# First MLP of a two-layer trunk: 22 of 32 up units by seven block products, h kept in DRAM, conditioning in wide pieces beside down

## The chip, the core and the metric

The kernel runs on one core of one Trainium2 chip. The metric is the device time of one execution in microseconds (us). The kernel before took 2450.26 us, the median of three runs (2447.16 to 2452.15). Below, PE is the matrix engine, DVE the vector engine, ACT the scalar engine, POOL the GpSimd engine and SP the engine that issues the transfers.

## What is computed

One inference step of a trunk of two layers on 1056 tokens (1024 of a prompt, 32 of a sample) with a model width of 1024. Layer 0 is an mLSTM mixer, layer 1 an attention over a band of keys that are computed once; each is followed by a squared-ReLU MLP of 4096 hidden units. Shift, scale and gate of every part come from a conditioning vector `c`, one for the prompt and one for the sample. Cut to what matters here:

```
def trunk(x, c, ...):
    for l in range(DEPTH):
        sh1, sc1, g1, sh2, sc2, g2 = jnp.split(ada_mod(c, p['w_ada'][l], p['b_ada'][l])[:, None, :], 6, axis=-1)
        u = x * (1 + sc1) + sh1
...
            kv_shift, kv_scale = jnp.split(ada_mod(c, p['w_ada_kv'], p['b_ada_kv'])[:, None, :], 2, axis=-1)
            kv = (x * (1 + kv_scale) + kv_shift) @ p['w_kv']
            q = (u @ p['w_q_b'][lb]).reshape(Bsz, S, NH_B, HD_B)
...
        x = layer_norm(ALPHA * x + (1 + g1) * y, p['ln_g'][l, 0], p['ln_b'][l, 0])
        u = x * (1 + sc2) + sh2
        f = jnp.square(jax.nn.relu(u @ p['w_up'][l])) @ p['w_down'][l]
        x = layer_norm(ALPHA * x + (1 + g2) * f, p['ln_g'][l, 1], p['ln_b'][l, 1])
```

So the queries and keys of layer 1 need the norm behind the first MLP, and that norm's output is modulated by the conditioning of layer 1 (`w_ada[1]`, 48 columns of 128) and of the keys and values (`w_ada_kv`, 16 columns).

## The kernel before

All data lie with the 1024 features on 128 partitions by 8 (`KC`), tokens along the free axis. Tokens are cut into three blocks of 384, 384 and 288 (`TBS`), or into four quarters of 264 (`QN`). A product in fp32 is made of three matmuls on numbers split into a high and a low part: high times high, high times low, low times high (`proj`, L118 to L120). ACT writes the high part of a weight block and DVE the low part (`split`, L89 and L90); the split weights lie in a ring of six slots ("wc"), the raw ones in a ring of three ("raw"). `U` holds the split, modulated input of the current stage.

**The first MLP** is `mlp` in `make_layer`. The 4096 hidden units are taken in 8 groups of 512. Up of group g+1 is interleaved with down of group g. An up tile is 24 matmuls into a PSUM bank; ACT and DVE take relu, square and split it (L1025 to L1028), and h stays in SBUF. A down tile is 12 matmuls; DVE adds it with the gate to the residual `acc`, which lies in one tile for each block of tokens (`add_gated_at`, L986). In the last group the block of 384 tokens comes first, then three up tiles that were kept back, then the other two blocks; when a block is complete, its norm starts (`norm`, L864 to L896), whose last step writes the block's part of `U` (L331) for the q projection.

**The conditioning** of layer 1 is `ada_cols`: 32 steps of two columns. A step loads two pieces of 512 KB, multiplies and adds them on DVE in rows of 256 (L238 and L241, 14 and 2 of them), transposes (L245) and sums (L246) on DVE; every fourth step PE sums across the partitions (L252). A `Flow` hands out these steps beside the matmuls: every tile "ticks" it by a share of its width, and `finish` runs what is left at once. The conditioning begins with the third block's first up tile and is finished ahead of the first block's norm.

**The second MLP** is already `mlp7`: of its 32 units of 256 hidden units by 528 tokens, 22 are computed by seven products of half blocks in place of eight (`Seven`, L1300, 12 matmuls each of 264 columns), ten plainly (four tiles of 24 matmuls); the sums and differences that this needs are made by DVE and ACT (`forms`, L1303 to L1310), and h goes through DRAM (`hd`). Its down is also made of such products (L1409).

The order of the instructions on each engine is fixed when the program is built; an engine runs its own in that order.

## Time and profile before

| what | value |
|---|---|
| median of three runs | 2450.26 us |
| the profiled execution's own time | 2451.64 us |
| its span in the trace | 2449.7 us |
| granted TensorE clock, mean | 0.993 |
| PE busy | 2386.9 us |
| DVE busy | 1919.8 us |
| ACT busy | 1090.7 us |
| moved by DMA | 335.15 MB |
| first MLP, from its first up matmul to the first q matmul | 518.4 to 1266.9 us |
| first up matmul of the second MLP | 1730.8 us |

Rows of the trace read so: a group has the line, the engine, the operation, the tile written and the tiles read with their shapes, and how often; then its busy time and the mean of one in ns; then how long the engine stood idle ahead of it and what ended that. A window's row has the window, its length and, for each engine, the busy time with the number of instructions; then the mean granted clock, the busy share of the DMA engines and GB/s.

### The profile page before, as it was taken

What the parts mean: (1) busy time and instruction counts of PE and PEld (TensorE: products, weight loads), DVE (VectorE), ACT (ScalarE), POOL (GpSimd) and SP (SyncE); (2) the same over time, 40 slices, a digit from 0 to 9 for tenths busy, and PEclk for the clock granted to TensorE, in tenths of its full rate; (3) what the DMA queues carried; (4) which work ended last, traced back from release to release, by engine and by line L of the source; (5) the groups of instructions that cost most, each with busy time, mean ns of one, the idle gap of its engine ahead of it and who ended that gap; (6) DMA issues with size and microseconds to landing.
All of it is one profiled execution on the core that took longest, in us unless ns stands there. A gap on an engine that the chain in (4) does not pass through costs nothing.

```text
span 2449.7 us, 42910 instructions
## 1 busy us (share of the span) xinstructions
PE 2386.9 (97%) x16580; PEld 2294.7 (94%) x16580; DVE 1919.8 (78%) x4340; ACT 1090.7 (45%) x2264; POOL 167.3 (7%) x315
## 2 busy tenths in 40 slices
PE   7999999999999999999999999999999999899997
PEld 4999999999999999999999977789999999899997
DVE  4899998788678678687488666755998888887878
ACT  4554456283212212212157466763776777222212
POOL 0211100000000000000000224420000000000003
PEclk9999999999999999999999999999999999999999
DMA  7432223412233233233223230041486779966642
GB/s 287 137 102 88 89 80 109 157 35 87 89 101 121 87 104 113 82 116 107 89 77 101 64 73 2 10 117 42 159 275 233 255 256 335 376 234 230 228 156 72
DMA packets 251503, 335.15 MB, mean 137 GB/s; under 512 B 12824, under 2 KB 201644, under 8 KB 250276
## 3 DMA queue, kind: packets, MB, share of 16 engines
q1 hardware_dynamic: 251300, 332.42, 41.4%
q8 instruction: 130, 2.13, 0.4%
q14 instruction: 73, 0.60, 0.1%
HBM read 255.50 MB, written 79.24 MB: 137 GB/s over the span
## 4 chain that ended last, share of the span: by engine, by line
PE 76%; DVE 12%; DMA 4%; ACT 3%; issue 2%; POOL 0%; SPq 0%; ACTq 0%; DVEq 0%; POOLq 0%
PE dn L1409 11%; PE up L1300 6%; PE up L118 6%; PE up L120 6%; PE up L119 6%; PE dn L119 5%; PE dn L118 5%; PE dn L120 5%; PE pv L1749 3%; PE s L1692 2%; PE pt L1727 2%; PE o L118 1%; PE o L119 1%; PE o L120 1%; DMA hd<-HL 1%
## 5 line engine op out<-in xcount | busy, mean ns | idle before, releaser
L1409 PE MATMUL dn<-fx,wf_d 128*128 128x264 f32 x2016 | 254.2, 285 | 6.9 <-DVE ACX L986 3.3
L1409 PEld LDWEIGHTS dn<-fx,wf_d 128*128 128x128 f32 x2016 | 248.7, 188 | 9.3 <-issue 2.9
L119 PE MATMUL dn<-h,w_dn 128*128 128x384 f32 (+1 forms) x768 | 249.5, 325 | 0.0
L118 PE MATMUL up<-U,w_up 128*128 128x384 f32 (+1 forms) x768 | 249.2, 324 | 0.0
L119 PE MATMUL up<-U,w_up 128*128 128x384 f32 (+1 forms) x768 | 247.9, 323 | 0.0
L118 PE MATMUL dn<-h,w_dn 128*128 128x384 f32 (+1 forms) x768 | 247.8, 323 | 0.0
L120 PE MATMUL up<-U,w_up 128*128 128x384 f32 (+1 forms) x768 | 247.6, 322 | 0.0
L120 PE MATMUL dn<-h,w_dn 128*128 128x384 f32 (+1 forms) x768 | 247.3, 322 | 0.0
L986 DVE SCALAR_TENSOR_TENSOR ACX<-dn,ada,ACX 128x264 f32<-128x264 f32 (+5 forms) x400 | 160.1, 426 | 52.6 <-PE dn L1409 39.6
L238 DVE SCALAR_TENSOR_TENSOR aacc<-rada,cs,aacc 128x256 f32<-128x256 f32 x448 | 190.1, 476 | 0.0
L986 DVE SCALAR_TENSOR_TENSOR acc<-dn,ada,acc 128x384 f32<-128x384 f32 (+2 forms) x256 | 119.2, 485 | 47.0 <-PE dn L120 45.6
L1025 ACT ACTIVATE r<-up 128x384 f32<-128x384 f32 (+1 forms) x96 | 44.3, 463 | 243.3 <-PE up L120 236.9
L119 PEld LDWEIGHTS dn<-h,w_dn 128*128 128x128 f32 x768 | 144.5, 188 | 0.2 <-DVE h L1028 0.2
L120 PEld LDWEIGHTS dn<-h,w_dn 128*128 128x128 f32 x768 | 144.5, 188 | 0.0
L120 PEld LDWEIGHTS up<-U,w_up 128*128 128x128 f32 x768 | 144.3, 188 | 0.0
L118 PEld LDWEIGHTS up<-U,w_up 128*128 128x128 f32 x768 | 144.2, 188 | 0.1
L119 PEld LDWEIGHTS up<-U,w_up 128*128 128x128 f32 x768 | 144.2, 188 | 0.0
L118 PEld LDWEIGHTS dn<-h,w_dn 128*128 128x128 f32 x768 | 143.9, 187 | 0.2
L1300 PE MATMUL up<-u,wf_u 128*128 128x264 f32 x1056 | 139.6, 284 | 1.3 <-ACT wf_u L89 0.6
L1300 PEld LDWEIGHTS up<-u,wf_u 128*128 128x128 f32 x1056 | 132.6, 188 | 1.9 <-ACT wf_u L89 0.8
L1027 DVE TENSOR_TENSOR r<-r 128x384 f32<-128x384 f32 (+1 forms) x96 | 49.9, 522 | 103.3 <-ACT h L1026 102.9
L89 ACT CAST w_up<-raw_up 128x1024 fp32r<-128x1024 f32 x52 | 54.3, 1046 | 136.4 <-DMA raw_up<-in_w_up_dram 102.5
(386 smaller groups left out, 6575.0 us busy)
## 6 DMA issues: line engine op xcount, KB each, us to landing
rada<-in_w_ada_dram SPq DMA_DIRECT2D x64, 512.0 KB
hd<-HL SPq DMA_DIRECT2D x28, 1056.0 KB
raw_up<-in_w_up_dram SPq DMA_DIRECT2D x52, 512.0 KB
fx<-hd SPq DMA_DIRECT2D x50, 528.0 KB
hd<-HM SPq DMA_DIRECT2D x28, 792.0 KB
raw_dn<-in_w_down_dram SPq DMA_DIRECT2D x36, 512.0 KB
ada_room<-in_w_ada_dram SPq DMA_DIRECT2D x32, 512.0 KB
rdn_u<-in_w_up_dram SPq DMA_DIRECT2D x32, 512.0 KB
```

The source lines that it names most:

```text
L89: nc.scalar.copy(dst_h, src)
L118: nc.tensor.matmul(ps, wh, mov(0, k), start=(k == 0), stop=False)
L119: nc.tensor.matmul(ps, wh, mov(1, k), start=False, stop=False)
L120: nc.tensor.matmul(ps, wl, mov(0, k), start=False, stop=(k == nk - 1))
L238: nc.vector.scalar_tensor_tensor(acc[:, cnd], raw[:, k], sc, acc[:, cnd], op0=ALU.mult, op1=ALU.add)
L986: nc.vector.scalar_tensor_tensor(xs, ps[:, off + o:off + o + mm_], gate[:, fc, cnd:cnd + 1], xs, op0=ALU.mult, op1=ALU.add)
L1027: nc.vector.tensor_mul(r, r, r)
L1300: nc.tensor.matmul(p, self.ws[w][:, wl, k], moving(f, tp, xl, k), start=first and k + n_ == 0, stop=k == 3 and n_ == 2, skip_group_check=n ...
L1409: nc.tensor.matmul(p, ws[w][:, wl, k], t[:, s0, xl], start=first and k + n_ == 0, stop=k == kg - 1 and n_ == 2, skip_group_check=not first)
L1692: nc.tensor.matmul(s[:, b, :w], qst, kk[i][:, g, k0 + j0:k0 + j0 + w], start=(i == 0), stop=(i == 1))
L1727: nc.tensor.transpose(pt[:kp, j - j0, pr * P:(pr + 1) * P], ps_[pr][:, j * P:j * P + kp], ident)
L1749: nc.tensor.matmul(pv[64 * e:64 * e + 64, :nq], V[:kp, vt0 + j, g * 64:(g + 1) * 64], pts[e][:kp, j, :nq], start=(j == 0), stop=(j == nt - 1))
```

## The change

- `mlp` is gone. The first MLP runs by `mlp7(L0)` with `nw = 0`. All of up comes first: ten units plainly (the hidden blocks 6 to 15 on the first 528 tokens, 40 tiles of 24 matmuls of 264 columns), 22 units by seven products of 12 matmuls.
- Every h is written to DRAM (`hpl0`) and read again: for five of the eight groups of down into strips of `U`, for the other three (1, 4, 7) into tiles of a pool of their own (`hs`).
- Down is plain, eight groups (the hidden blocks in the order 0, 3, 1, 4, 2, 5, 7, 6): five of them in quarters of 264 tokens, three in the blocks of 384, 384 and 288. In the last group the loop runs over the blocks outside, and each block's norm follows its last tile. No up tile is left by then.
- The residual is two tiles of four feature rows over all tokens (`Halves`). It goes to DRAM (`xsp[3]`) after the norm ahead of the MLP and is loaded again (`reload`, tiles `ACX`), because scratch of the seven products lies in its place.
- Conditioning: eight columns of `w_ada_kv` stay narrow and run beside the seven products (`ada_some`). The 48 columns of `w_ada[1]` and the other eight of `w_ada_kv` run beside down in `ada_wide`: 14 steps of four columns, rows of 512, two pieces of 1 MB a step, which take slots of the "wc" ring. `finish` stands ahead of the first block's norm again.

```diff
+    def ada_wide(src, c0, base, nch, mk, tmp_f, raw_f, step):
+        for j in range(0, nch, 4):
+            acc = [tmp_f([P, 512], f"aw_{base}_{j}_{cnd}") for cnd in range(2)]
+            for half in range(2):
+                raw = raw_f([P, 4, 512], f"radw_{base}_{j}_{half}")
...
+                yield step[0]
+                for k in range(4):
+                    for cnd in range(2):
+                        sc = cs[:, 4 * half + k, cnd:cnd + 1]
+                        if half or k:
+                            nc.vector.scalar_tensor_tensor(acc[cnd], raw[:, k], sc, acc[cnd], op0=ALU.mult, op1=ALU.add)
+                        else:
+                            nc.vector.tensor_scalar(acc[cnd], raw[:, k], sc, None, op0=ALU.mult)
...
+        if not NW:
+            L.reload(3)
+            L.down()
+            for c in range(4):
+                h_load(1, c)
+            for g in range(8):
+                if g < 7:
+                    for pr in range(4):
+                        w_plain(g, pr)
+                        if g < 6 and pr:
+                            for c in ((0, 1), (2,), (3,))[pr - 1]:
+                                h_load(g + 2, c)
+                        for fc in (2 * pr, 2 * pr + 1):
+                            for t0, n in TBS if g % 3 == 1 else blocks_p:
+                                dn_plain(g, fc, t0, n)
+                else:
+                    for pr in range(4):
+                        w_plain(g, pr)
+                    for t0, n in L.blocks:
+                        for fc in range(KC):
+                            dn_plain(g, fc, t0, n)
+                        L.after((t0, n))
...
+    def ada_some():
+        yield from ada_cols(a["w_ada_kv"], 0, 96, 8, mm, tmp_t, ADA_B)
     def ada_rest():
-        yield from ada_cols(a["w_ada"][1], 0, 48, 48, mm, tmp_t, ADA_B)
-        yield from ada_cols(a["w_ada_kv"], 0, 96, 16, mm, tmp_t, ADA_B)
+        yield from ada_wide(a["w_ada"][1], 0, 48, 48, mm, tmp_t, wc_tile, ADA_W)
+        yield from ada_wide(a["w_ada_kv"], D, 104, 8, mm, tmp_t, wc_tile, ADA_W)
...
-    mlp(hp, 0, ada_part(0, 5), fwd, before0, end0, TBS)
...
+        def after(blk):
+            t0, n = blk
+            ti = TBS.index(blk)
+            flow.finish(norms["ada"])
+            norms[ti] = flow.add(norm(ti, 1, f"n01_{ti}", W01, False, lambda ti: acc_dma(
+                xsp[1][:, :, t0:t0 + n], acc[ti], True)), now=NOW)
+    mlp7(L0)
```

**First place: DVE at the end of the first MLP.** Before, the last rows of the conditioning (`aacc_96_14` is the last step's sum) stand beside the down tiles of group 6 (`dn_0_6_…`, group, feature row, first token):

```order
L986 SCALAR_TENSOR_TENSOR acc0_2_5244<-dn_0_6_1_768_12063,ada_87,acc0_2_5244 128x32
L238 SCALAR_TENSOR_TENSOR aacc_96_14_12028<-rada_96_14_1_12101,cs_86,aacc_96_14_12028 128x256 x4
L986 SCALAR_TENSOR_TENSOR acc0_0_5252<-dn_0_6_2_0_12083,ada_87,acc0_0_5252 128x384
L245 STREAM_TRANSPOSE aat_96_14_12168<-aacc_96_14_12028 128x512
L90 TENSOR_TENSOR w_dn0_6_2_12211<-raw_dn0_6_2_12209,w_dn0_6_2_12211 128x1024
L986 SCALAR_TENSOR_TENSOR acc0_1_5248<-dn_0_6_2_384_12103,ada_87,acc0_1_5248 128x384
L246 TENSOR_REDUCE cx_117<-aat_96_14_12168 128x16
```

Also before, a group later on DVE, the first block's norm (`s_n01_0` is its first sum) stands among and right behind that block's last adds, and relu and split of an up tile follow (`r`, `h`):

```order
L867 TENSOR_TENSOR s_n01_0_12724<-acc0_0_5252 128x768
L986 SCALAR_TENSOR_TENSOR acc0_0_5252<-dn_0_7_4_0_12663,ada_87,acc0_0_5252 128x384
L986 SCALAR_TENSOR_TENSOR acc0_0_5252<-dn_0_7_5_0_12677,ada_87,acc0_0_5252 128x384
L869 TENSOR_TENSOR s_n01_0_12724<-s_n01_0_12724,acc0_0_5252 128x768
L986 SCALAR_TENSOR_TENSOR acc0_0_5252<-dn_0_7_6_0_12696,ada_87,acc0_0_5252 128x384
L986 SCALAR_TENSOR_TENSOR acc0_0_5252<-dn_0_7_7_0_12710,ada_87,acc0_0_5252 128x384
L869 TENSOR_TENSOR s_n01_0_12724<-s_n01_0_12724,acc0_0_5252 128x768
L870 TENSOR_TENSOR s_n01_0_12724<-s_n01_0_12724 128x384
L90 TENSOR_TENSOR sr_n01_0_12729<-s_n01_0_12724,sr_n01_0_12729 128x384
L1027 TENSOR_TENSOR r_0_7_3_384_12757<-r_0_7_3_384_12757 128x384
L1028 TENSOR_TENSOR h_0_7_3_12556<-r_0_7_3_384_12757,h_0_7_3_12556 128x384
```

Now, on DVE, the two last conditioning steps (`aw_104_0` and `aw_104_4`, of `w_ada_kv`) begin behind an add of the last group's third block (tokens from 768):

```order
L1034 SCALAR_TENSOR_TENSOR ACX0_0_9705<-dn0_7_3_768_14367,ada_88,ACX0_0_9705 128x256
L1034 SCALAR_TENSOR_TENSOR ACX0_0_9705<-dn0_7_3_768_14367,ada_88,ACX0_0_9705 128x32
L267 TENSOR_SCALAR aw_104_0_0_13995<-radw_104_0_0_13997,cs_87 128x512
L267 TENSOR_SCALAR aw_104_0_1_13996<-radw_104_0_0_13997,cs_87 128x512
L265 SCALAR_TENSOR_TENSOR aw_104_0_0_13995<-radw_104_0_0_13997,cs_87,aw_104_0_0_13995 128x512
L265 SCALAR_TENSOR_TENSOR aw_104_0_1_13996<-radw_104_0_0_13997,cs_87,aw_104_0_1_13996 128x512
```

and only when both are through does the first block's norm begin:

```order
L272 STREAM_TRANSPOSE awt_104_4_0_14115<-aw_104_4_0_14093 128x512
L272 STREAM_TRANSPOSE awt_104_4_1_14118<-aw_104_4_1_14094 128x512
L274 TENSOR_REDUCE cx_118<-awt_104_4_0_14115 128x2x8
L274 TENSOR_REDUCE cx_118<-awt_104_4_1_14118 128x2x8
L915 TENSOR_TENSOR s_n01_0_14152<-ACX0_0_9705 128x768
L288 TENSOR_TENSOR ada_88<-adas_104_6_14121,pt2_86 128x16
L917 TENSOR_TENSOR s_n01_0_14152<-s_n01_0_14152,ACX0_1_10391 128x768
L299 TENSOR_SCALAR ada_88<-ada_88 128x16
L1034 SCALAR_TENSOR_TENSOR ACX0_1_10391<-dn0_7_5_768_14428,ada_88,ACX0_1_10391 128x256
```

Between the first of these rows and the norm's first stand 40 rows of the two steps: 28 of L265, four of L267, four transposes, four sums. So the end of the conditioning moved from a group ahead of the norm to directly ahead of it, behind nearly all the adds of all three blocks.

**Second place: PE at the same point.** Before, the first mean of the norm stands between up tiles that were kept back:

```order
L119 MATMUL up_0_7_2_768_12762<-U_133,w_up0_7_1_1_12498 128x288
L120 MATMUL up_0_7_2_768_12762<-U_133,w_up0_7_1_1_12498 128x288
L864 MATMUL mean_n01_0_12792<-sr_n01_0_12729,ones_d_73 128x384 x2
L118 MATMUL up_0_7_3_768_12814<-U_133,w_up0_7_1_0_12493 128x288
L119 MATMUL up_0_7_3_768_12814<-U_133,w_up0_7_1_0_12493 128x288
```

Now, on PE, the conditioning's sums over partitions (`adas_104_6`) and the mean stand behind the tile `dn0_7_6_768`:

```order
L119 MATMUL dn0_7_6_768_14452<-hs_0_7_3_13263,w_dn0_7_3_13934 128x288
L120 MATMUL dn0_7_6_768_14452<-hs_0_7_3_13263,w_dn0_7_3_13934 128x288
L285 MATMUL adas_104_6_14121<-cx_118,sel_69 32x16 x4
L912 MATMUL mean_n01_0_14202<-sr_n01_0_14157,ones_d_73 128x384
L118 MATMUL dn0_7_6_384_14266<-hs_0_7_0_13001,w_dn0_7_3_13934 128x384
L912 MATMUL mean_n01_0_14202<-sr_n01_0_14157,ones_d_73 128x384
```

Behind `adas_104_6` the matmuls left of the first MLP are those of three tiles, `dn0_7_6_384`, `dn0_7_4_768` and `dn0_7_7_768`, 36 in all; between the add's tile `dn0_7_3_768` and `adas_104_6` there are two tiles, `dn0_7_5_768` and `dn0_7_6_768`, 24 matmuls.

**Third place: DVE at the start of down.** The low half of the weights of feature rows 4 and 5 of group 0 (`w_dn0_0_2`) now stands behind all adds of row 3, and PE's next tile reads it:

```order
L1034 SCALAR_TENSOR_TENSOR ACX0_0_9705<-dn0_0_3_264_10618,ada_88,ACX0_0_9705 128x264
L1034 SCALAR_TENSOR_TENSOR ACX0_0_9705<-dn0_0_3_528_10636,ada_88,ACX0_0_9705 128x264
L1034 SCALAR_TENSOR_TENSOR ACX0_0_9705<-dn0_0_3_792_10650,ada_88,ACX0_0_9705 128x232
L1034 SCALAR_TENSOR_TENSOR ACX0_0_9705<-dn0_0_3_792_10650,ada_88,ACX0_0_9705 128x32
L90 TENSOR_TENSOR w_dn0_0_2_10667<-raw_dn0_0_2_10665,w_dn0_0_2_10667 128x1024
L1034 SCALAR_TENSOR_TENSOR ACX0_1_10391<-dn0_0_4_0_10672,ada_88,ACX0_1_10391 128x264
```

There is no such place in before, whose first down tiles have up tiles between them; the same order holds once more for `w_dn0_0_3` behind the adds of row 5. In the groups from 2 on, the weights stand two to ten tiles ahead.

313 lines of the change are left out of this document (161 added, 152 removed).

## The prediction

> **What bounds the kernel now.** I read the page's busy times and the chain of work that ended last first:
>
> ```profile
> span 2449.7 us, 42910 instructions
> PE 2386.9 (97%) x16580; PEld 2294.7 (94%) x16580; DVE 1919.8 (78%) x4340; ACT 1090.7 (45%) x2264; POOL 167.3 (7%) x315
> PE 76%; DVE 12%; DMA 4%; ACT 3%; issue 2%; POOL 0%; SPq 0%; ACTq 0%; DVEq 0%; POOLq 0%
> ```
>
> PE is the bound over the whole, but a share of 97% says nothing of one stage. So next come the windows of the first MLP, and the rows of its matmuls and of the first q matmuls behind it:
>
> ```profile
> 518.30:1266.80 748.50, 748.46 (x4683) 746.09 (x4683) 555.64 (x1194) 203.93 (x354) 0.00 (x0) 1.00 0.30 93
> L118 PE MATMUL up<-U,w_up x768: 288/336/443, 518.4 to 1236.0; 128*128 128x384 f32 x128, 128*128 128x288 f32 x64
> L118 PE MATMUL dn<-h,w_dn x768: 292/334/443, 577.0 to 1266.5; 128*128 128x384 f32 x128, 128*128 128x288 f32 x64
> L118 PE MATMUL q<-U,w_q x192: 288/336/447, 1266.9 to 1362.3; 128*128 128x384 f32 x128, 128*128 128x288 f32 x64
> ```
>
> In this stage PE is busy for 748.46 of 748.50 us, at full clock, with DVE at 555.64 (74%). Nothing waits: the stage costs exactly its matmuls, and the first q matmul starts 0.4 us after the last down matmul. What the change can gain here is matmul columns only, and every wait that it makes is new. With three lines each of 768 matmuls, up has 2304 and down 2304, of 352 columns on average, in all 1,622,000 columns in 748.5 us: **0.4615 ns a column**, so 121.8 ns for one of 264.
>
> The end of the stage matters as much. The waits of PE from 1200 to 1420 us (microseconds in all, times, longest), then three rows of DVE's timeline (start, duration) of the first block's norm:
>
> ```profile
> PE kv L1644 <- DVE uk L90: 3.0, 3, 1.9
> PE q L118 <- DVE QO L1573: 0.5, 1, 0.5
> PE q L118 <- ACT U L326: 0.2, 1, 0.2
> ```
>
> ```profile
> 1226.30 0.96 DVE L869 TENSOR_TENSOR s_n<-s_n,acc 128x768 f32<-128x768 f32 x1
> ...
> 1253.52 0.56 DVE L331 TENSOR_TENSOR U<-ut_n,U 128x384 fp32r<-128x384 f32 x1
> ...
> 1267.72 0.55 DVE L331 TENSOR_TENSOR U<-ut_n,U 128x384 fp32r<-128x384 f32 x1
> ```
>
> From the block's last sum to the first row of `U` pass 27.2 us, to the last 41.4 us, and PE hardly waits (0.7 us ahead of q), since it has three up tiles and two blocks of group 7 to do meanwhile. That cover is what I look for in the changed order.
>
> **Up, by columns.** Ten plain units have 10 × 4 tiles × 24 = 960 matmuls, 22 units of seven products have 22 × 7 × 12 = 1848, that is 84 a unit in place of 96. In all 2808 of 264 columns: 2808 × 0.1218 = 342.0 us, against 2304 × 352 × 0.4615 ns = 374.3 before: **−32.3**. Down keeps its columns, 374.3 us.
>
> **Up, by waits.** The second MLP has exactly this stage already:
>
> ```profile
> 1725.00:1854.00 129.00, 122.00 (x973) 120.86 (x973) 125.46 (x169) 94.26 (x150) 0.00 (x0) 0.99 0.67 226
> 1854.00:2083.50 229.50, 227.92 (x1863) 226.87 (x1862) 201.55 (x347) 165.80 (x290) 0.00 (x0) 1.00 0.79 272
> ```
>
> It takes 358.5 us, 16.5 over its columns, 7.0 of them idle PE in the first window, where DVE is busy for 125 of 129 us. Here DVE has less to do beside the products: h is only split, with no differences of h to form, and the conditioning beside them is four narrow steps. I take +5, between 0 and that stage's 16.5, nearer to the low end as the first window's idle comes of a full DVE. That h goes through DRAM I cost at nothing: the second window moves 272 GB/s at a share of 0.79 with PE idle for 1.6 us of 229.5.
>
> **Down, by waits.** DVE now carries twelve of the fourteen wide steps here. The rows for their prices:
>
> ```profile
> L238 DVE SCALAR_TENSOR_TENSOR aacc<-rada,cs,aacc 128x256 f32<-128x256 f32 x448 | 190.1, 476 | 0.0
> L241 DVE TENSOR_SCALAR aacc<-rada,cs 128x256 f32<-128x256 f32 x64 | 19.9, 342 | 0.0
> L245 DVE STREAM_TRANSPOSE aat<-aacc 128x512 f32<-128x512 f32 x32 | 22.6, 705 | 0.3
> L246 DVE TENSOR_REDUCE cx<-aat 128x16 f32<-128x512 f32 x32 | 21.7, 678 | 0.2
> L986 DVE SCALAR_TENSOR_TENSOR acc<-dn,ada,acc 128x384 f32<-128x384 f32 x128 | 78.3, 612 | 35.1 <-PE dn L120 34.1
> L986 DVE SCALAR_TENSOR_TENSOR ACX<-dn,ada,ACX 128x264 f32<-128x264 f32 x200 | 96.7, 488 | 31.0 <-PE dn L1409 28.2
> L90 DVE TENSOR_TENSOR w_dn<-raw_dn,w_dn 128x1024 fp32r<-128x1024 f32 x36 | 43.6, 1213 | 15.4 <-ACT w_dn L89 15.4
> ```
>
> No row has 512 columns with a scalar from `cs`. From 264 to 384 columns the same operation gains 124 ns, 1.03 ns a column, so 512 take 744 ns alone; in a run, 448 rows of 476 ns took 190.1 us, 424 each, so 52 ns of each hide under its neighbour: 692 ns. A wide step is 14 × 0.692 + 2 × 0.45 (L241's price, with another 256 columns) + 2 × 0.705 + 2 × 0.68 = 13.4 us, two steps 26.7; without overlap 28.4. In 6.3 groups of down (295 us of PE) DVE's order has twelve steps (160 us), 29 weight splits (35) and some 240 adds (92 with the same overlap), 287 us: **97% full**, where this stage had 74%. In such a stretch the second MLP's first window lost 7 us of 129. Most of DVE's work here is not urgent, though, so I take +4, from 0 to 15. At the start of down two weight splits stand behind adds of the tile just ahead of their first use: one split of ACT and DVE, some 2 us of PE each, **+4** (0 to 6).
>
> **The tail.** This is the term that decides. In DVE's order the two last conditioning steps stand behind the add of `dn0_7_3_768`, and the norm's first row behind them. What PE still has in that time is two tiles, 24 matmuls of 288 columns, 3.2 us. Then it stands at `adas_104_6`, which needs the second step's sums. Add 0.6 us, two steps 26.7 to 28.4 us, less 3.2: **24.4 us** of idle PE (24 to 26). In before these rows cost nothing, since a whole group of matmuls covered them.
>
> Then the norm of the first block starts, 45 DVE rows up to the first `U`. Its wide rows:
>
> ```profile
> L877 DVE TENSOR_TENSOR acc<-acc,mean_n 128x768 f32<-128x768 f32 x16 | 14.5, 947 | 2.4 <-PE mean_n L864 2.4
> L881 DVE TENSOR_TENSOR q_n<-q_n,q_n 128x768 f32<-128x768 f32 x18 | 17.1, 952 | 0.2
> L896 DVE TENSOR_TENSOR acc<-acc,w_n 128x768 f32<-128x768 f32 x16 | 14.9, 950 | 0.0
> ```
>
> There are 19 such rows (0.95 us each, 18.1), since the second block's sums and centring stand between; five weight splits for q at 1.21 (6.1); and small rows and adds, some 9 at the prices above. With the overlap of some 50 ns a row that is 30 us, and some 2 for the ways from DVE to ACT and PE and back. It agrees with the 27.2 us of before's timeline. PE's cover is 36 matmuls (12 × 177 + 24 × 133 ns = 5.3 us) and the norm's own, 1: **+26** (22 to 30). The rest of `U` comes over another 11 us, in which PE can take only the rows that are there, and the second block's over 21 more, which five or six q tiles of 4.2 us cover: **+4** (2 to 8).
>
> And PE that waited comes back slow:
>
> ```profile
> PE var_n L864 <- ACT qr_n L89: 4.1, 1, 4.1
> 1700.00:1750.00 50.00, 45.91 (x299) 45.45 (x298) 46.70 (x89) 35.90 (x70) 0.00 (x0) 0.97 0.28 87
> ```
>
> After the one wait of 4.1 us the window's granted clock is 0.97, 1.5 us of 50. The tail ends with waits at least that long: +1.5. [...]
>
> Tail: 24.4 + 26 + 4 + 1.5 = **56** (50 to 62).
>
> **Sum.** −32.3 + 5 + 4 + 4 + 56 = +36.7 on the profiled execution's 2451.64: **2488 us**. The median shown is 1.4 lower, which is within the runs' own spread.
>
> **Rivals.**
>
> *The tail is covered (faster).* If PE had matmuls for the tail as in before, with 4 us of waits between 1200 and 1420, the sum would be −32.3 + 13 + 4 = −15, 2436 us. The point from which it decides: the tail's idle under 19 us, the gain less the other waits. For it speaks that before hid the same 27 us of norm nearly whole. Against it: the orders are fixed, and with 60 matmuls behind that add the two steps alone pass 19 us. Chance 0.04.
>
> *Only the conditioning is paid.* If the norm's chain runs shorter and the three tiles left cover more of it (a tail of 30 in place of 56), the sum is +11, 2462. Against it stands that the norm's rows have prices seen twice, in groups and timeline. Chance 0.08.
>
> *DVE becomes the bound of down.* At 97% in a fixed order each late row delays the next add, PSUM banks stay taken and PE stops: +15 in place of 4, and up at the second MLP's 16.5: 2488 + 11.5 + 11 = 2511; with the one alone 2499. For it: the window with DVE at 125 of 129. Chance 0.15.
>
> *The products don't save what they should.* If forms and splits come too late all through, up loses 32 in place of 5 and is no faster than before: 2515. Against it, the second MLP's later window is 99% busy. Chance 0.05.
>
> The forecast itself: 0.68.
>
> **How the numbers follow.** The lowest bounds of all terms give 2451.64 − 32.3 + 50 = 2469, the highest 2451.64 − 32.3 + 16.5 + 15 + 6 + 62 = 2519; that all are at their highest is unlikely, and with one of the waits of up and down at its middle it is 2512. I give 2468 to 2512, which leaves out the covered tail, the conditioning alone and half of the fourth rival, some 0.15, and a little of the third. About 0.2% (5 us) is what a measurement of this kernel can tell from no change. Faster by more than that: 0.04. Within it: 0.03, a tail between the two first rivals. Slower: 0.93.
>
> **What would show it.** In the changed kernel's trace: a gap of PE of some 24 us at `adas`, released by DVE, and then waits for the mean, the variance and `U` of 20 to 30 us in all between the last down matmuls and q; DVE busy without a gap in that time, first with rows of 512, then of 768. Up from its first matmul to the first of down some 347 us with PE over 98% busy. Down some 380 us. I am wrong on the tail if DVE is idle in it, or if PE's gap there is under 40 us; wrong on down if PE waits for adds through all its groups; wrong on up if waits for split weights sum to over 15 us.

## The result, and the profile after

The changed kernel takes **2485.2 us** (median of 4 runs, 2481.8 to 2487.7), the kernel before in the same series 2449.2 (4 runs, 2447.2 to 2452.2): a ratio of **1.0148, 95% interval 1.0133 to 1.0163**, so 1.5% slower. The forecast was 2488 with a range of 2468 to 2512. The profiled execution took 2483.62 us (before: 2451.64).

Its page, the same rows as those shown of before: span, busy times, and the shares of the chain that ended last.

```profile
span 2481.8 us, 45295 instructions
PE 2367.8 (95%) x17564; PEld 2274.1 (92%) x17564; DVE 1994.5 (80%) x4254; ACT 1179.6 (48%) x2394; POOL 167.0 (7%) x315
PE 46%; DVE 13%; DMA 5%; ACT 4%; issue 2%; SPq 1%; POOL 0%; DVEq 0%; ACTq 0%; POOLq 0%
```

PE is busy for 19 us less than before, and the span is 32 us longer: some 51 us more in which PE does nothing. The rows of the first MLP's matmuls and of the first q matmuls say between which times to look:

```profile
L118 PE MATMUL up<-U,w_up x320: 280/285/289, 513.4 to 630.6; 128*128 128x264 f32 x160
L118 PE MATMUL dn<-U,w_dn x640: 278/285/586, 862.2 to 1200.7; 128*128 128x264 f32 x160
L118 PE MATMUL q<-U,w_q x192: 288/336/686, 1295.1 to 1393.6; 128*128 128x384 f32 x128, 128*128 128x288 f32 x64
```

From the first up matmul to the first of q pass 781.7 us; before it was 748.5. By the windows (PE, PEld, DVE, ACT, POOL busy, then clock, DMA share and GB/s) this is up, all of down but its end, the start of down, and the tail:

```profile
513.40:862.20 348.80, 345.36 (x2822) 343.16 (x2821) 275.20 (x441) 239.20 (x420) 0.00 (x0) 1.00 0.64 208
862.20:1237.00 374.80, 367.31 (x2756) 365.24 (x2755) 300.60 (x578) 34.77 (x35) 0.00 (x0) 0.99 0.61 211
862.20:909.00 46.80, 39.31 (x307) 38.53 (x305) 27.50 (x54) 4.89 (x6) 0.00 (x0) 0.95 1.01 370
1243.00:1295.10 52.10, 12.03 (x50) 10.75 (x50) 50.66 (x83) 13.33 (x18) 0.00 (x0) 0.59 0.24 78
```

Up is the gain, 348.8 us where before's columns took 374.3, with PE idle for 3.4 us. Down loses 7.5 us of idle PE, all of it in the third window, its first 47 us, where the DMA engines are at a share of 1.01. The loss is the last window: 52.1 us in which DVE is busy for 50.7 and PE for 12.0, at a granted clock of 0.59. The waits of PE from 1238 to 1400 us name its parts:

```profile
PE adas L285 <- DVE cx L274: 22.4, 1, 22.4
PE var_n L912 <- ACT qr_n L89: 7.5, 1, 7.5
PE mean_n L912 <- ACT sr_n L89: 5.7, 2, 4.1
PE q L118 <- ACT U L359: 5.6, 2, 4.7
```

And DVE's timeline in that time (start, duration, how many in a row; a bracket would show idle time ahead of a row):

```profile
1239.60 0.64 DVE L1034 SCALAR_TENSOR_TENSOR ACX<-dn,ada,ACX 128x256 f32<-128x256 f32 x2 [0.94 <-PE dn L120]
1240.16 0.88 DVE L267 TENSOR_SCALAR aw<-radw,cs 128x512 f32<-128x512 f32 x2
1240.95 9.36 DVE L265 SCALAR_TENSOR_TENSOR aw<-radw,cs,aw 128x512 f32<-128x512 f32 x14
...
1253.39 9.36 DVE L265 SCALAR_TENSOR_TENSOR aw<-radw,cs,aw 128x512 f32<-128x512 f32 x14
...
1265.04 0.95 DVE L915 TENSOR_TENSOR s_n<-ACX 128x768 f32<-128x768 f32 x1
...
1296.00 0.55 DVE L364 TENSOR_TENSOR U<-ut_n,U 128x384 fp32r<-128x384 f32 x1
```

The add of `dn0_7_3_768` ends at 1240.2, the two steps run without a gap to 1265.0 (24.9 us), and then the norm's first row starts; the first row that writes its low half of `U` starts 31.0 us later. PE has three tiles for all of this.

Why the two steps come so late can be read on DVE and SP just ahead of the tail:

```profile
1191.00:1243.00 52.00, 51.74 (x344) 51.22 (x343) 19.04 (x41) 0.00 (x0) 0.00 (x0) 1.00 0.21 74
1189.55 50.41 SPq L258 DMA_DIRECT2D radw<-in_w_ada_kv_dram  x4
```

DVE is busy for 19 of these 52 us, almost only with adds, each of which waits for its matmuls. The four pieces of the two steps are issued at 1189.6, 1201.3, 1236.4 and 1239.6 us, and SP stands for 34.7 us ahead of the third until a `dn` matmul (L120) of PE releases it. The pieces take slots of the ring "wc", where the split weights of the last group lie until PE has read them.

### The profile page after: what moved, and what is told of

Read it like the earlier page. It is cut to its first block, busy times and chain, and to the rows that moved or that the text cites. A ratio compares the mean times of both kernels' runs of the same rounds, so it can differ in the third digit from the quotient of the medians.

```text
span 2481.8 us, 45295 instructions
## 1 busy us (share of the span) xinstructions
PE 2367.8 (95%) x17564; PEld 2274.1 (92%) x17564; DVE 1994.5 (80%) x4254; ACT 1179.6 (48%) x2394; POOL 167.0 (7%) x315
## 3 DMA queue, kind: packets, MB, share of 16 engines
q1 hardware_dynamic: 298340, 420.78, 50.7%
## 4 chain that ended last, share of the span: by engine, by line
PE 46%; DVE 13%; DMA 5%; ACT 4%; issue 2%; SPq 1%; POOL 0%; DVEq 0%; ACTq 0%; POOLq 0%
PE dn L1407 11%; PE up L1269 5%; PE dn L120 5%; PE dn L118 5%; PE dn L119 5%; PE pv L1838 3%; PE s L1781 2%; PE pt L1816 2%; DVE wf_u L90 2%; DMA rdn_u<-in_w_up_dram 1%; PE q L118 1%; DVE HL L90 1%; PE q L119 1%; PE q L120 1%; PE op_b L118 1%
## 5 line engine op out<-in xcount | busy, mean ns | idle before, releaser
L1034 DVE SCALAR_TENSOR_TENSOR ACX<-dn,ada,ACX 128x264 f32<-128x264 f32 (+6 forms) x696 | 288.5, 437 | 122.9 <-PE dn L120 74.2
L118 PE MATMUL dn<-U,w_dn 128*128 128x264 f32 x640 | 183.9, 287 | 6.0 <-DVE ACX L1034 6.0
L119 PE MATMUL dn<-U,w_dn 128*128 128x264 f32 x640 | 182.8, 286 | 0.0
L120 PE MATMUL dn<-U,w_dn 128*128 128x264 f32 x640 | 181.0, 285 | 1.5 <-DVE w_dn L90 1.5
L1269 PE MATMUL up<-TF,wf_u 128*128 128x264 f32 x1056 | 143.3, 285 | 2.1 <-ACT H L1272 2.1
L265 DVE SCALAR_TENSOR_TENSOR aw<-radw,cs,aw 128x512 f32<-128x512 f32 x196 | 138.9, 745 | 7.9 <-DMA radw<-in_w_ada_dram 7.9
L1269 PE MATMUL up<-U,wf_u 128*128 128x264 f32 x1056 | 139.6, 285 | 1.1 <-ACT H L1272 0.5
L1269 PEld LDWEIGHTS up<-TF,wf_u 128*128 128x128 f32 x1056 | 134.2, 188 | 3.0 <-ACT H L1272 2.7
L1269 PEld LDWEIGHTS up<-U,wf_u 128*128 128x128 f32 x1056 | 133.1, 188 | 2.2 <-DVE H L1275 1.4
L118 PE MATMUL dn<-hs,w_dn 128*128 128x384 f32 (+2 forms) x416 | 131.9, 317 | 0.0
L119 PE MATMUL dn<-hs,w_dn 128*128 128x384 f32 (+2 forms) x416 | 131.3, 316 | 0.0
L120 PE MATMUL dn<-hs,w_dn 128*128 128x384 f32 (+2 forms) x416 | 130.7, 314 | 0.0
L118 PEld LDWEIGHTS dn<-U,w_dn 128*128 128x128 f32 x640 | 121.7, 190 | 6.4 <-DVE ACX L1034 6.2
L120 PEld LDWEIGHTS dn<-U,w_dn 128*128 128x128 f32 x640 | 120.3, 189 | 2.0 <-DVE w_dn L90 2.0
L119 PEld LDWEIGHTS dn<-U,w_dn 128*128 128x128 f32 x640 | 122.1, 191 | 0.0
L238 DVE SCALAR_TENSOR_TENSOR ada_room<-ada_room,cs 128x256 f32<-128x256 f32 x224 | 99.7, 480 | 3.3 <-DMA ada_room<-in_w_ada_dram 3.3
L120 PE MATMUL up<-u,w_up 128*128 128x264 f32 x320 | 92.4, 290 | 3.0 <-DVE w_up L90 3.0
```

The lines of the kernel that those rows point to most:

```text
L118: nc.tensor.matmul(ps, wh, mov(0, k), start=(k == 0), stop=False)
L119: nc.tensor.matmul(ps, wh, mov(1, k), start=False, stop=False)
L120: nc.tensor.matmul(ps, wl, mov(0, k), start=False, stop=(k == nk - 1))
L238: nc.vector.scalar_tensor_tensor(acc[:, cnd], raw[:, k], sc, acc[:, cnd], op0=ALU.mult, op1=ALU.add)
L265: nc.vector.scalar_tensor_tensor(acc[cnd], raw[:, k], sc, acc[cnd], op0=ALU.mult, op1=ALU.add)
L1034: nc.vector.scalar_tensor_tensor(xs, ps[:, off + o:off + o + mm_], gate[:, fc, cnd:cnd + 1], xs, op0=ALU.mult, op1=ALU.add)
```

## The experiments

Two theories of the tail stood against each other at the start. **Place:** the two last conditioning steps cost what they cost since no matmuls are left beside them; beside matmuls their 24.9 us are free. **DVE time:** DVE has no 25 us to spare anywhere from up to q, so moving them moves the loss. Each run is read by the same stages, in us; "up" is from the first up matmul to the first down matmul, "down" from there to the first q matmul, "q" the first to the last L118 matmul of q. The fifth column of numbers is the sum of the three against the eighth run, in which the two steps are left out. These columns are read from one execution of each kernel, and that can lie some us off the kernel's median: the eighth run's is 4.1 us below its median, the first's 3.4 and the tenth's 3.5 above. So the last column gives the median time of the whole kernel less the median of before in the same series.

| kernel | up | down | up + down | q | against the 8th | median, against before |
|---|---|---|---|---|---|---|
| before | | | 748.5 | 95.4 | +7.8 | 0 |
| changed | 348.8 | 432.9 | 781.7 | 98.5 | +44.1 | +36.0 |
| 1 last two steps by the other ring | 350.1 | 388.1 | 738.2 | 116.4 | +18.5 | +9.1 |
| 2 finish ahead of group 7 | 349.7 | 408.8 | 758.5 | 101.6 | +24.0 | +16.7 |
| 3 kv beside the products | 357.6 | 405.3 | 762.9 | 99.6 | +26.4 | +16.8 |
| 4 h loads spread | 348.1 | 428.8 | 776.9 | 99.0 | +39.8 | +34.0 |
| 5 as 3, paced | 363.4 | 398.6 | 762.0 | 101.8 | +27.7 | +21.8 |
| 6 as 5, h loads spread | 364.2 | 394.0 | 758.2 | 102.0 | +24.1 | +17.2 |
| 7 before, four narrow steps late | | | 758.1 | 125.0 | +47.0 | +40.9 |
| 8 two steps left out | 349.6 | 386.2 | 735.8 | 100.3 | 0 | −7.9 |
| 9 two steps beside q | 348.5 | 386.7 | 735.2 | 118.0 | +17.1 | +8.2 |
| 10 as 9, h loads spread | 351.9 | 384.6 | 736.5 | 117.0 | +17.4 | +7.5 |
| 11 kv from the plain up tiles on | 369.4 | 388.3 | 757.7 | 99.6 | +21.2 | +13.4 |
| 12 as 1, finished ahead of group 7, h loads spread | 349.5 | 396.2 | 745.7 | 102.9 | +12.5 | +9.3 |

**1. The last two steps through the other ring.** Their pieces take the raw weights' ring, in 512 KB instead of 1 MB, so they can be loaded and used beside group 6.

```diff
-        yield from ada_wide(a["w_ada_kv"], D, 104, 8, mm, tmp_t, wc_tile, ADA_W)
+        yield from ada_wide_raw(a["w_ada_kv"], D, 104, 8, mm, tmp_t, ADA_W)
```

> The changed kernel, but the pieces of the two last wide steps (w_ada_kv) come in four pieces of 512 KB through the ring of the raw weights, and not in two of 1 MB through the ring of the split weights; rows, widths, pace and place in the program are the same. Theory (the ring puts the steps at the tail, and with them the norm behind all adds): the steps run beside group 6, the first block's norm stands among the adds of the second block again, PE's wait at adas falls from 22.4 us to under 3, its waits for mean, variance and U from 23 us to under 6, down itself stays within 3 us: 2436 us (2431 to 2442). Rival (DVE is full, the steps are late for want of room on it): the rows delay adds of group 6 and PE waits for these instead, 20 us of the gain come back: 2455 or more. Rival (the norm's chain is uncovered anyway since no up tile is left): only the 22 us at adas go, 2461.

Measured: 2456.7 us, ratio 1.0034 (1.0022 to 1.0047). The tail is gone as expected: no wait for `cx`, up and down together 43.5 us shorter, and down no slower for it. But 18 of these are given back in q. PE's longest wait from 1190 to 1400 us, and the windows of down, of the stretch ahead of the tail that was shown above, and of q:

```profile
PE var_n L939 <- ACT qr_n L89: 14.6, 2, 12.3
```

```profile
862.00:1253.00 391.00, 381.91 (x2867) 379.43 (x2866) 350.98 (x666) 49.10 (x57) 0.00 (x0) 0.99 0.62 215
...
1191.00:1243.00 52.00, 52.00 (x351) 51.43 (x350) 48.59 (x92) 7.10 (x9) 0.00 (x0) 1.00 0.30 98
...
1253.70:1370.10 116.40, 98.39 (x581) 96.27 (x580) 79.95 (x147) 71.10 (x144) 6.05 (x3) 0.93 0.30 91
```

From 1191 to 1243 us, where DVE was idle for 33 us in the changed kernel, it now does the rows of the steps, and PE is busy for all 52 us. In q DVE is busy for 80 of 116 us, so it isn't full over this stage: PE stands for 12.3 us at the third block's variance, which in this kernel's order comes ahead of q tiles whose weights DVE splits late. During that one wait DVE is busy for 11.3 of the 12.3 us, mostly with rows of the norms. Place explains most of the tail, not where the 18 us came from.

**2. The conditioning finished ahead of group 7.** Only the place of `finish` changes.

```diff
+        def ended():
+            flow.finish(norms["ada"])
         def after(blk):
-            flow.finish(norms["ada"])
...
                 else:
+                    L.ended()
                     for pr in range(4):
```

> The changed kernel, but what is left of the conditioning is finished ahead of the last group of down and not ahead of the first norm; the ring stays. In DVE's order one and a half steps then stand between the adds of group 6 and the weight splits of group 7, and the norm among the adds of the second block. It parts the tail in two. Theory: PE waits some 20 us at the border of groups 6 and 7, as it did at adas, but the norm is covered again by two blocks of down (30 us): about 25 us of the tail go, 2458 us (2452 to 2464), with waits for mean, variance and U of under 6 us in all. Rival (norm uncovered anyway): the wait only moves, 2480 or more. Rival (all of the loss is the conditioning's place): 2440 or less.

Measured: 2464.2, ratio 1.0064 (1.0049 to 1.0079). Two rows of PE's waits, the span over:

```profile
PE adas L285 <- DVE cx L274: 19.0, 1, 19.0
PE var_n L912 <- ACT qr_n L89: 4.1, 1, 4.1
```

The wait for the two steps goes along to the border of groups 6 and 7, and is 3 us shorter; the norm is covered by group 7 again. So of the two steps' 44 us, 20 belong to the norm that stood behind the steps, and 24 to the steps themselves.

**3. The eight columns narrow, beside the products.**

```diff
-        yield from ada_cols(a["w_ada_kv"], 0, 96, 8, mm, tmp_t, ADA_B)
+        yield from ada_cols(a["w_ada_kv"], 0, 96, 16, mm, tmp_t, ADA_B)
...
-        yield from ada_wide(a["w_ada_kv"], D, 104, 8, mm, tmp_t, wc_tile, ADA_W)
```

> The changed kernel, but all sixteen columns of w_ada_kv are narrow steps beside the seven products; the two wide steps at the end are gone. Theory: no conditioning stands at the tail and the norm is covered, as with the other ring; four more narrow steps (32 us of DVE rows) go into the up stage, where DVE is busy 275 of 349 us, and cost 0 to 3 us there: 2437 us (2431 to 2443). Rival (DVE's load decides): the up stage grows by 10 us or more.

Measured: 2464.4, ratio 1.0065 (1.0047 to 1.0083), far from the 2437 expected. Two rows of PE's waits:

```profile
PE adas L285 <- DVE cx L246: 13.0, 1, 13.0
PE dn L118 <- ACT w_dn L89: 6.2, 1, 6.2
```

The flow didn't get through its steps during the products; the rest was forced at the start of down, where PE waited for it and for weights behind it.

**4. The loads of h spread over group 0.** Group 1's loads of h are issued one after each pair of feature rows in place of four at the start.

```diff
-            for c in range(4):
-                h_load(1, c)
...
+                        if g == 0:
+                            h_load(1, pr)
```

> The changed kernel, but the 4.3 MB of h for group 1 of down are asked for one by one behind each pair of feature rows of group 0, and not all at the start of down. The tail stays as it is. Theory: at the start of down the second half of the first wide step's weights landed 17 us after its issue, in a stretch where the DMA engines were busy without a gap; DVE stood 7.3 us at it with adds queued behind it, and PE waited 6.0 us for these. With 4.3 MB less in the queues the piece lands in time: PE's wait for adds at the start of down goes, 2477 us (2474 to 2480). Rival (the reloads of the residual and of group 0 alone fill the queues): the wait stays, 2482 to 2486. Rival (h of group 1 now comes late): a wait for hs at the start of group 1.

Measured: 2481.5, ratio 1.0134 (1.0119 to 1.0149), with down 4.1 us shorter in the profiled execution. The medians of the whole, each against before in its own series, differ by only 2.0, and the two intervals overlap, so the gain in time isn't resolved; the wait is. In the changed kernel, PE's one wait for an add in down is this, from 862 to 1238 us:

```profile
PE dn L118 <- DVE ACX L1034: 6.0, 1, 6.0
```

DVE's and SP's timelines show how it comes about. SP issues the second half of the first wide step at 879.95, behind loads of h; DVE stands at its rows until 896.98, with the adds of down behind them:

```profile
889.15 0.49 DVE L1034 SCALAR_TENSOR_TENSOR ACX<-dn,ada,ACX 128x264 f32<-128x264 f32 x1 [1.58 <-PE dn L120]
896.98 5.39 DVE L265 SCALAR_TENSOR_TENSOR aw<-radw,cs,aw 128x512 f32<-128x512 f32 x8 [7.33 <-DMA radw<-in_w_ada_dram]
```

```profile
879.95 0.48 SPq L258 DMA_DIRECT2D radw<-in_w_ada_dram  x1
881.27 8.48 SPq L1330 DMA_DIRECT2D U<-hpl  x2
```

With the loads spread the same piece is used 11 us after its issue in place of 17, DVE stands at it for 2.0 us, and of the 6.0 us the last row is left, while the waits for split weights grow from 1.5 us:

```profile
PE dn L120 <- DVE w_dn L90: 3.2, 2, 2.7
PE dn L118 <- DVE ACX L1034: 0.7, 1, 0.7
```

**5 and 6. As the third, paced so that the steps are through by down; then with h spread too.** One chain for all of the conditioning, a pace of 300 in place of 480.

```diff
-        l, nw, pace, alloc, add, gate = 0, 0, 480, mm, add_gated_at, ada_part(0, 5)
+        l, nw, pace, alloc, add, gate = 0, 0, 300, mm, add_gated_at, ada_part(0, 5)
...
     def ada_rest():
+        yield from ada_some()
...
         def seven():
-            norms["ada"] = flow.add(ada_some())
+            norms["ada"] = flow.add(ada_rest())
         def down():
-            flow.finish(norms["ada"])
-            norms["ada"] = flow.add(ada_rest())
+            pass
```

> As the third experiment (all of w_ada_kv narrow beside the seven products), but with a faster pace there (one unit of the flow for 300 columns and not 480) and with nothing finished by force at the start of down: the conditioning is one chain that runs on into down. In the order its last step stands beside group 6, the norm among the adds of the second block, the weights of q ahead of the second block's centring. Theory (the tail is the ring's doing, and what the first and third experiments kept of it came from the weights of q that the pieces held up, and from the forced finish at the start of down): no wait at adas above 2 us, waits for mean, variance and U at the tail under 8 us in all, 2440 us (2434 to 2446), below the kernel before. Rival (DVE, 96% busy through down, decides, and the time comes back wherever the rows stand): 2455 or more.

> The fifth experiment with the h of group 1 asked for pair by pair as in the fourth. Theory: the two are independent, so 3 to 4 us less than the fifth: 2436 us (2430 to 2442). Rival (the wait at the start of down moves to another piece once the tail is gone): the same as the fifth.

Measured: 2469.0, ratio 1.0087 (1.0074 to 1.0101), and 2464.3, ratio 1.0068 (1.0055 to 1.0081). The level is missed by some 29 us, the step from one to the other (4.6) is a little more than the 3 to 4 expected. In the fifth run no wait for `cx` is left, but up is 14.6 us longer, and down begins with

```profile
PE dn L118 <- ACT w_dn L89: 14.8, 1, 14.8
```

because ACT waits for a piece of the raw weights. SP issues it at 903.0 us, behind loads of h and a wide piece; it is used 18.6 us later, and from 903 to 918 us the DMA engines are at a share of 1.02. With h spread the wait is 9.2. That the conditioning's narrow pieces, which go through the same ring as the raw weights, make it late was not shown apart from this. The 44 us of the two steps became 28, in the products and in this wait.

**7. The kernel before, with only its conditioning made late.** None of the change, but the last eight columns of `w_ada_kv`, four narrow steps, are held back until `finish`.

```diff
-        yield from ada_cols(a["w_ada_kv"], 0, 96, 16, mm, tmp_t, ADA_B)
+        yield from ada_cols(a["w_ada_kv"], 0, 96, 8, mm, tmp_t, ADA_B)
+        yield 1e9
+        yield from ada_cols(a["w_ada_kv"], D, 104, 8, mm, tmp_t, ADA_B)
```

> The kernel before, with the last four narrow steps of its conditioning (32 us of DVE rows) held back to the finish ahead of the first block's norm, as late as in the changed kernel. In DVE's order the last two of them (16 us) stand behind the first block's adds; PE has three up tiles and sixteen down tiles behind them, 40 us. Theory (late steps cost what PE has no matmuls for): 16 us of rows and 27 us of norm against 40 us of matmuls, so under 2 us of wait at adas and some 3 to 12 us in all, since in PE's order the norms of the second and third block now stand ahead of most q tiles: 2456 us (2450 to 2462). Rival (a late finish costs its rows wherever it stands): 2470 or more.

Measured: 2488.1, ratio 1.0164 (1.0150 to 1.0178), where 2456 was expected. Waits of PE from 1190 to 1400 us, and the window of q:

```profile
PE var_n L864 <- ACT qr_n L89: 14.3, 2, 12.1
PE mean_n L864 <- ACT sr_n L89: 7.7, 2, 5.0
PE adas L252 <- DVE cx L246: 7.1, 1, 7.1
```

```profile
1273.60:1398.60 125.00, 101.00 (x596) 98.34 (x595) 82.95 (x152) 69.73 (x142) 5.76 (x3) 0.88 0.29 91
```

Lateness alone, without the products, the wide rows or h through DRAM, costs the kernel before 39 us (883.1 against 843.9 for the three stages), as much as the whole change. Up tiles were still there as cover, and held the direct wait to 7 us; the rest comes by the norms of the second and third block, which PE now meets ahead of q tiles. DVE is busy for 83 of 125 us in q (76 of 95 in before), so over the stage it isn't full: this points to order, not to DVE's time.

**8. The two steps left out.**

```diff
-        yield from ada_wide(a["w_ada_kv"], D, 104, 8, mm, tmp_t, wc_tile, ADA_W)
+        nc.vector.memset(ada[:, 104:112, :], 0.0)
```

> The changed kernel without its two last wide steps: the eight columns of w_ada_kv that scale the keys' input are left out (zeros stand for them), nothing is put in their place. It prices the tail alone, without what the first, third and fifth experiments moved into the rings and the up stage. Theory (the two steps and the norm that they hold back are the tail, and the rest of the change gains): from the first up matmul to the first q matmul 738 us, as with the other ring, q itself 98 to 102 us, since its weights are split in time: 2440 us (2434 to 2446), below the kernel before. Rival (q's stage is longer by itself after this change, whatever stands ahead of it): q 110 us or more, 2455.

This kernel leaves out a part of what is to be computed: zeros stand for the eight columns. Measured: 2441.1, ratio 0.9967 (0.9955 to 0.9978). This is the size of the term: with two steps of fourteen gone, up and down are 45.9 us shorter, and the rest of the change gains 8 us on the kernel before. Of PE's waits there, from 862 to 1238 and from 1190 to 1400 us, these rows show that the one at the start of down stays and that the tail is gone:

```profile
PE dn L118 <- DVE ACX L1034: 5.7, 1, 5.7
```

```profile
PE var_n L912 <- ACT qr_n L89: 2.1, 1, 2.1
PE q L118 <- ACT U L359: 1.6, 1, 1.6
```

**9 and 10. The two steps beside q; then with h spread too.** They are needed for the keys and values only, behind q. Their pieces go through the raw ring as in the first run.

```diff
-        yield from ada_wide(a["w_ada_kv"], D, 104, 8, mm, tmp_t, wc_tile, ADA_W)
...
+    def ada_late():
+        yield from ada_wide_raw(a["w_ada_kv"], D, 104, 8, mm, tmp_t, (4.0, 4.0, 4.0))
+        ada_fix(96, [(1, "sc")])
+    norms["kv"] = flow.add(ada_late())
     for gi, grp in enumerate(((0, 1, 2), (3,))):
...
+    flow.finish(norms["kv"])
     kvss = cp.tile([P, 2, KC, 2], F32, name="kvss")
```

> The changed kernel with the two last wide steps, which only the keys and values need, moved behind the norm's start, beside the q projection, in four pieces each through the ring of the raw weights; the norm no longer waits for them. Theory: start to first q 738 us as without them; DVE, busy some 76 of 96 us beside q, takes 27 us more and has room for most of it there and beside the keys: 2444 us (2437 to 2451). Rival (DVE is full there too, and q's evictions wait): 2460 or more.

> The ninth experiment with the h of group 1 asked for pair by pair as in the fourth. Theory: 3 to 4 us less than the ninth, 2440 us (2433 to 2447). Rival (the wait moves elsewhere): the same as the ninth.

Measured: 2457.1, ratio 1.0037 (1.0025 to 1.0049), and 2456.5, ratio 1.0031 (1.0019 to 1.0043). PE waits for the steps for only 1.0 us (at `adas`), and up and down are as in the eighth run, but q is 18 us longer:

```profile
1248.70:1366.70 118.00, 103.97 (x589) 97.46 (x588) 104.62 (x193) 67.49 (x140) 6.20 (x3) 0.94 0.37 118
```

Here DVE is busy for 104.6 of 118 us, where the eighth run has 81.1 of 100.3: its 23.5 us more became 17.7 of time, in many short waits, most of them for DVE's rows of `QO` (the split of q's output) and for `U`. The chain of work that ended last, followed through this stage, has the steps' rows (L294) for 11.7% and PE's q matmuls for 12.5%; in the eighth run the q matmuls have 85.7% of it. This is DVE's time as the second theory has it. That spreading h saves 3 to 4 us more here isn't resolved: the two medians differ by 0.7.

**11. The eight columns narrow, begun beside the plain up tiles.** DVE is busy for 90.8 of 117.8 us there in the changed kernel. The pace is 300 as in the fifth run, and h is spread.

```diff
-        yield from ada_cols(a["w_ada_kv"], 0, 96, 8, mm, tmp_t, ADA_B)
+        yield from ada_cols(a["w_ada_kv"], 0, 96, 16, mm, tmp_t, (8.0, 4.0, 2.0, 8.0))
...
+            if i == 1:
+                norms["ada"] = flow.add(ada_some())
```

> The last sixteen columns of kv's conditioning go through the narrow steps of the first eighty, and this chain is started ahead of the second of the plain up tiles instead of at the start of down, with shares of work per step of 8, 4, 2 and 8 and a pace of 300; the loads of h are spread as in the fourth run. Theory (the two steps cost what the stage that takes them lacks in free DVE time: 45 us uncovered behind down, 24 at the border of groups 6 and 7, 18 to 20 beside group 6 or q, 15 to 26 beside up): the plain up tiles have more free DVE time than any of these stages, so the steps cost less there: up 350 to 356 us, start of the products to the start of q 738 to 746 (735.8 with the steps left out, 781.7 in the changed kernel), q 99 to 102, time 2440 to 2450, that is, level with the kernel before or a little faster. Rival (DVE is full from up to q wherever the steps stand, or the raw weights of down come late behind the conditioning's pieces as in the fifth and sixth runs): start to q 752 or more, with waits for w_dn at the start of down, and 2457 or more.

Measured: 2462.0, ratio 1.0050 (1.0037 to 1.0064), which is the rival's number. The plain tiles pay only 4 us for what DVE does more there, but the products pay 16, and the start of down waits for its weights. The longest of PE's waits from 637 to 900 and from 900 to 1380 us:

```profile
PE up L1269 <- DVE H L1275: 5.9, 5, 3.5
PE up L1269 <- ACT H L1272: 3.3, 3, 1.7
```

```profile
PE dn L118 <- ACT w_dn L89: 7.0, 1, 7.0
```

**12. The first run with `finish` ahead of group 7, and h spread.** The edits of the first, second and fourth run together. In DVE's order the two steps now stand among the adds of group 6, and the weights of q ahead of where the first run had them.

> The first run's edit (the last two wide steps in pieces of 512 KB through the raw ring, beside group 6) with two more: what is left of the conditioning is finished ahead of group 7, as in the second run, and the loads of h are spread, as in the fourth. In the order of DVE both steps now stand among the adds of group 6, with one product row, two transposes and two sums left over at the border, and the weights of q are split ahead of where the first run had them; on PE the norm's rows of the third block stand behind more q tiles than there. Theory (the first run's 18 us in the q stage came from the order there, the late weights of q and the norm ahead of the q tiles, and not from DVE's time as such): q 100 to 103 us in place of the first run's 116.4; from the start of the products to the start of q 736 to 746 (738.2 there, less up to 4 for the loads of h, plus up to 10 for a wait at the border of groups 6 and 7); time 2438 to 2449, level with the kernel before or faster. Rival (the two steps' 25 us of DVE rows cost 17 to 28 us wherever they stand, as in every run so far): the 16 us saved at q come back ahead of it, start to q 752 or more, or q stays at 114 or more; time 2453 to 2460.

Measured: 2455.6, ratio 1.0037 (1.0023 to 1.0051). Both are partly right. q is 102.9 us and up with down 745.7, as the theory said, so the first run's loss in q came from the order there. But 7.5 us of it came back in up and down, and the first and the twelfth run lose the same against before, 9.1 and 9.3. Its time of 2438 to 2449 is missed: 5 us stand at the border again and others at weights of down (the longest of PE's waits from 513 to 1400 us):

```profile
PE adas L312 <- DVE cx L301: 4.8, 1, 4.8
PE dn L120 <- DVE w_dn L90: 4.6, 3, 2.7
```

By the stages it is the cheapest place found, 12.5 us for the two steps; by the medians it is not. The first, ninth, tenth and twelfth run stand within 1.6 us of one another, and none beats the kernel before.

**What stands.** The two steps cost 44 us in the changed kernel, by the stages and by the medians (36.0 more than before, where the eighth run has 7.9 less). At the four best places they cost 12.5 to 18.5 by the stages and 15 to 17 by the medians. So some 27 us are place: about 20 the norm behind them (second run), the rest their own rows once matmuls stand beside them. For the tail the second theory is wrong, since DVE was idle for 33 of the 52 us ahead of it; the first run, which changes only the ring and the size of the pieces, moves the rows there, and PE doesn't wait for them in that stretch. At least 12 us by the stages, and 15 by the medians, stayed at every place tried. That they are DVE's time is shown beside q, in the one execution profiled (ninth run). Beside up and at the border the runs show displaced rows and late weights as well, and don't separate these. Whether an earlier place, ahead of the first MLP, would be free was not tried.

## Why the prediction was right, point by point

- **Up, by columns and waits:** right. −32.3 of columns and +5 of waits were forecast, 347 us; it took 348.8, a loss of 6.8 over 342.0. Half of it (3.4) is idle PE, in short waits for ACT and DVE to take the products from PSUM (`H`, L1272 and L1275); the rest is busy time above the columns' worth.
- **Down, DVE full and late splits:** the sum was too small, 8 forecast, 11.6 measured: from 862.2 to the wait at 1242.8 pass 380.6 us, for columns worth 374.3 less the 5.3 of the three tiles left. And its parts were elsewhere. The late splits cost 1.5 in place of 4 (`dn L120` waiting for `w_dn` twice). That DVE would be 97% full came true for 188 us of it, but the 4 us of waits for this did not:

```profile
909.00:956.00 47.00, 47.00 (x311) 46.72 (x312) 44.47 (x82) 6.30 (x6) 0.00 (x0) 0.98 0.71 234
956.00:1003.00 47.00, 47.00 (x374) 46.83 (x372) 45.86 (x86) 5.15 (x5) 0.00 (x0) 1.00 0.68 243
1003.00:1050.00 47.00, 47.00 (x394) 46.82 (x393) 45.52 (x87) 4.15 (x5) 0.00 (x0) 1.00 0.70 238
1050.00:1097.00 47.00, 47.00 (x321) 46.80 (x320) 45.89 (x83) 4.35 (x5) 0.00 (x0) 1.00 0.65 217
```

  In these 188 us DVE is busy for 181.7 and PE for all 188. In the first run DVE is busier over the whole stage than in the changed kernel, 351.0 of 391.0 us against 300.6 of 374.8, and down is only 2 us longer than with the steps left out. What down lost is 7.5 us of idle PE at its start, for the step named next and the late splits, and some 4 us of busy time above the columns' worth, with the granted clock at 0.95 in the first 47 us.
- **"That h goes through DRAM I cost at nothing":** this step failed. It was argued from a window of up with the DMA engines at a share of 0.79. At the start of down, h's reads and the wide pieces go out together, at a share of 1.01 and 370 GB/s, and a piece is used only 17 us after its issue; DVE waits for it in order, and the adds and PE behind it: 6.0 us, which spreading the loads cut to 0.7.
- **The tail:** the mechanism was right and the sum 6 too large, 56 forecast, 50 measured: 52.3 us from the wait to q, less 5.3 of matmuls, plus 3.1 by which q is longer.
  - The wait at `adas`: 22.4 in place of 24.4. Fourteen rows of 512 took 9.36 us, 669 ns each, where 692 was worked out; the mean duration of one in the trace is 745, and 744 was forecast.
  - The norm uncovered: from the end of that wait to q pass 29.9 us. Less the 6.3 us that the forecast had for the three tiles' matmuls and the norm's own, this is 23.6, where 26 and 1.5 for the slow clock were forecast. The chain was as long as thought (31.0 us from its first row to the low half of `U`, 32 forecast), but q starts on the high half, which ACT writes earlier (its first row starts at 1294.4 us, DVE's at 1296.0). The rest of `U` cost 3.1 by which q is longer, 4 forecast.
  - The slow clock: it was taken from a single wait, and more matmuls ran slow than that. With bursts of some 4 us between waits the granted clock is 0.59 over the whole window, and 50 matmuls take 241 ns each, 12.0 us of busy PE in place of 6.3. As time this cost little, though, since PE would else have waited for DVE, which is busy for 50.7 of the 52.1 us. It is seen at the start of q, at a clock of 0.50 for the first 4.6 us; over all of q PE is busy for 2.0 us more than before (96.8 against 94.7) at a clock of 0.97. In the first burst the matmuls of 384 columns start 320 ns apart for 3.1 us, and 174 behind that. The second burst of 4.1 us stays slow throughout, with 288 columns every 240 ns, so two bursts of 4.1 us each ran differently.
  - Two sums of the working are slightly off, and nothing hangs on them: by its prices two steps without overlap take 28.2 us, not 28.4, and the highest bounds of the tail's terms add up to 65.5, not 62.
- **Rivals.** That only the conditioning is paid (2462) is what the second run shows when the norm is covered again: 2464. That DVE becomes the bound of down didn't happen: full as it was, PE didn't stop. A part of it holds beside q, where DVE's time is the limit once the two steps stand there. But the point from which a tail would decide was set too high, at 19 us: without the steps the change gains only 8, and where they cost 12.5 to 18.5 (first, ninth and twelfth run) it loses 8 to 9. That is the losses of up and down again, 18.4 in place of 13, and a q that is 5 us longer than before even without the steps. That the products don't save didn't happen: up is the one stage that is shorter.

The forecast for the three stages together was +36.7, and they lost 36.3: up −25.5, down +11.6, tail +47.0, q +3.1. That these sums agree to 0.4 us is luck: up and down lost 5.4 more than forecast and the tail 5.9 less. Where the tail is and about how large it is was worked out. The whole execution lost only 32.0, as the changed kernel's first up matmul came 5.0 us earlier in that one run (513.4 against 518.4; the other kernels, with the same code ahead of it, have 513 to 517).

## What to carry to other kernels

A chain that everything later waits for is priced by what PE still has left behind the point where its last input comes, and not by its share of an engine: here 25 us of DVE rows, moved by one group, cost 44 us, and a like lateness alone cost the kernel before 39. Look also at what holds such a chain back: here DVE was idle for 33 us just ahead of the tail, while the loads of the late steps stood for ring slots until PE's matmuls released them. When work is moved to an engine that is 75 to 85% busy, look for the stage that takes it and for what it pushes back: late weight splits and norms two stages on were worth as much as the direct wait. Price a new stream of DMA at the stage where it meets the other streams, since here DVE stood 7.3 us at one late piece with adds of down queued behind it, and PE 6.0 us for these.

## What the runs showed of the hardware

- The granted clock of PE is 0.59 over 52 us with bursts of some 4 us between waits of 2 to 22 us; in the kernel before, with one wait of 4.1 us, it is 0.97 over 50 us. In the tail one burst had matmuls of 384 columns every 320 ns for its first 3.1 us and every 174 ns behind that; another had 288 columns every 240 ns for all of its 4.1 us, where just ahead of the tail they start every 132 ns.
- One operation has two prices: the SCALAR_TENSOR_TENSOR row of 128x512 in fp32 has a mean duration of 745 ns, and fourteen in an unbroken run take 9.36 us, 669 ns each, so neighbours overlap.
- With the DMA engines at a share of 1.01 and 370 GB/s, a piece of 1 MB was used 17 us after its issue; with 4.3 MB less asked for at that time, 11 us after.
- DVE busy for 181.7 of 188 us, beside down, cost PE nothing; DVE waiting 7.3 us for one late piece cost PE 6.0.
